# Sums of weight quarters for the feed-forwards' second matrices: from four VectorE additions to accumulating DMAs in DRAM, and three more tiles by seven products

## The chip, the core and the metric

The kernel runs on one core of a Trainium2 chip. Its time is device microseconds (us) from one launch; lower is better. Times below are either medians of several runs or come from one profiled execution, and it is said which.

## What is computed

A decoder layer for 512 tokens of width 1024, all in float32: a SwiGLU feed-forward (FFN1), a token mixer (HGRN2 and mLSTM heads), and a second feed-forward (FFN2), each between RMS norms and with a residual. Only the feed-forwards matter here:

```python
def swiglu_ffn(x, w_in, w_out):
    gate, up = jnp.split(x @ w_in, 2, axis=-1)
    return (jax.nn.silu(gate) * up) @ w_out        # (512, 2816) @ (2816, 1024)
...
    x = x + 0.5 * rms_norm(swiglu_ffn(rms_norm(x, norm_pre[l, 0]), ffn1_w_in[l], ffn1_w_out[l]), norm_post[l, 0])
    x = x + rms_norm(mixed, norm_post[l, 1])
    x = x + 0.5 * rms_norm(swiglu_ffn(rms_norm(x, norm_pre[l, 2]), ffn2_w_in[l], ffn2_w_out[l]), norm_post[l, 2])
```

## The kernel before

**Float32 by three matmuls.** Every float32 operand is split into a rounded high part and a low part (what is left). ScalarE (ACT) writes the high part with a copy, VectorE (DVE) the low part with a subtraction; `split` (L250, its instructions at L273 and L275) does this for each weight tile, `two_parts` (L812, L813) for each tile of activations. A product is then three matmuls: high by high, high by low, low by high.

**The second matrix (`ffn_out`, L858).** w_out has 2816 rows, taken in eleven pairs of 128 rows (k2 = 0 to 10), and 1024 columns, taken in two halves of 512. One tile is 256 rows by 512 columns, 512 KB. `OUT` gives the order of the pairs in each half; the last four (`LAST`) of the second half are done row chunk by row chunk, so that the norm after them can start early. A tile is done in one of two ways:

- *plain* (`plain`, L893): for each of four chunks of 128 tokens and each of two column quarters, two row halves by three matmuls of 128x256: 48 matmuls.
- *by quarters* (`product`, L901, called by `quartered`): the tile is taken as 2x2 quarters of 128 rows by 256 columns, and multiplied with seven products in place of eight (Strassen's scheme in Winograd's form), each of them two matmul columns by three matmuls: 42 matmuls. It needs four sums of the weight quarters and four sums of quarters of the activations. The activations' sums are DVE additions in `h_sums` (L844), split by `s_tile`; the plain quarters of the activations that it also needs are split by `h_quarters`. The weights' sums are four DVE additions of 128x256 in `sum_quarters` (L306), made in place in the loaded tile after its first split; then the tile is split a second time. So a quartered tile takes two entries of the list of weights, and its loaded buffer is held until the second one is split.

`QUARTERED` names the pairs done by quarters: six in the first half, four in the second. The products by quarters of one half go to four sums of their own (M), and `common` adds them to the results (C) once the last quartered tile of the half is done (L863); `post0` then takes the first half's results through square (ACT, L437), a small GpSimd (POOL) operation (L438) and a multiplication (DVE, L475).

**What sets the order.** All engines run their own queues in order. `weights` makes a due time for each load: a load can be issued when its ring buffer was read for the last time and not more than 8 entries ahead. Rings: `raw` with three buffers, `raw2` with five; all w_out tiles go through `raw2`. SyncE (SP) issues all loads in one queue (L236). `feed` keeps up to four split weight tiles (`WBUF`) ahead of TensorE (PE). Activations by quarters lie in the free buffers of the transposed input (`PLACES`), others in two of the three `raw` buffers. In `ffn_in` the first matrix goes through PE as products p1 to p7 of 24 matmuls each (L603); its weights are added up by DVE (L289) after their loads.

Of the kernel before, what the change touches and what calls it, by code (L numbers as in the profile page):

```python
# [8 lines left out]
F32 = mybir.dt.float32  # L9
F32R = mybir.dt.float32r  # L10
AF = mybir.ActivationFunctionType
ALU = mybir.AluOpType
PSUM = bass.MemoryType.PSUM

P = 128
T = 512
D = 1024
# [5 lines left out]
RAW, WBUF, PAD, LATE, NEXT, FRONT, STEP = 3, 4, 128, 112, 64, 96, 16  # L23
# [55 lines left out]

QUARTERED = [(2, 3, 4, 6, 7, 8), (2, 4, 6, 8)]
OUT = [list(range(PAIRS)), [9, 2, 4, 10, 6, 8, 0, 1, 3, 5, 7]]
LAST = 4
PLACES, LATER = {2: 1, 4: 2, 6: 0, 8: 3}, {0: (1, 0), 7: (2, 3)}

AGAIN, ROWS = (9, 10), (18, 19, 20, 21)

# [25 lines left out]
class Layer:  # L116
    def __init__(self, ctx, tc, aps):
        self.tc, self.nc = tc, tc.nc
        self.__dict__.update(aps)
        nc = self.nc  # L120
        pool = lambda name, **kw: ctx.enter_context(tc.tile_pool(name=name, bufs=1, **kw))
        self.cp, self.wp, self.sp, self.psp = pool("cp"), pool("wp"), pool("sp"), pool("psp", space=PSUM)
        self.uid, self.hold = 0, ()
        self.wt, self.free, self.slot = None, deque(), {}

        self.ident = self.cp.tile([P, P], F32, name="ident")
        make_identity(nc, self.ident)
        self.nhalf = self.cp.tile([P, 8], F32, name="nhalf")
        nc.gpsimd.memset(self.nhalf, -0.5)
        self.xs = self.cp.tile([P, NT, D], F32, name="xs")  # L130

        xq = {n: self.cp.tile([P, 2 * D + 2 * STEP * (n == 0)], F32R, name=f"xq{n}") for n in (1, 2, 3, 0)}
        self.xt = [xq[n] for n in range(4)]
        self.xq = [t[:, : 2 * D].rearrange("p (b k t) -> p b k t", b=2, k=KH) for t in self.xt]

        x0 = self.xt[0].rearrange("p (b x) -> p b x", b=2)[:, :, :D].rearrange("p b (k t) -> p b k t", k=KH)
        self.xh = [x0, *self.xq[1:]]
        self.prm = self.cp.tile([P, 36], F32, name="prm")

    def nm(self, s):  # L140
        self.uid += 1
# [108 lines left out]
    def split(self):  # L250

        nc = self.nc
        it = self.items.popleft()
        raw = self.raw[it.key]
        _, a, b = raw.shape
        if it.dst:
            w = it.dst()
        else:
            if self.wt is None:
                self.wt = self.wp.tile([P, 2 * D * WBUF + FRONT + PAD], F32R, name="w")  # L260
            if not self.slot and it.key[0] != "mix":
                self.free = deque(FREE2 if it.key[0] == "f2" else FREE)
            n, o = self.lie("out" if it.key[1] == "out" else "mix" if it.key[0] == "mix" and b == 512 else "any")
            self.free.remove(n)
            w = self.wt[:, o : o + 2 * D].rearrange("p (b k t) -> p b k t", b=2, k=a)
            self.slot[id(w)] = n, o, w
        hi, lo = self.both(w)
        if it.sums:
            raw, hi, lo = (self.flat(v)[:, QUARTER:] for v in (raw, hi, lo))
        self.ready.append((w, it.dst is not None))  # L270
        rows = it.rows
        if rows is None:
            nc.scalar.copy(hi, raw)  # L273
            yield
            self.low = nc.vector.tensor_tensor(lo, raw, hi.bitcast(F32), op=ALU.subtract)  # L275
        else:
            for j in range(a):
                nc.scalar.activation(hi[:, j], raw[:, j], AF.Copy, scale=rows[:, j : j + 1])
            yield
            for j in range(a):  # L280
                nc.vector.scalar_tensor_tensor(  # L281
                    lo[:, j], raw[:, j], rows[:, j : j + 1], hi[:, j].bitcast(F32), op0=ALU.mult, op1=ALU.subtract
                )
        with self.behind(*self.hold):
            for out, other in it.adds:
                o, c = self.raw[out], self.raw[other]

                late = out[1] >= (HEAD if out[0] == "f1" else 1)
                (nc.vector if late else nc.gpsimd).tensor_tensor(o, o, c, op=ALU.add)  # L289
        if it.sums:  # L290
            self.sum_quarters(self.quarters(self.raw[it.key]))
        self.load_due(self.done)
        self.done += 1
        yield
# [4 lines left out]
    def quarters(self, v):  # L299
        v = self.flat(v)  # L300
        return [v[:, QUARTER * j : QUARTER * (j + 1)] for j in range(4)]

    def sum_quarters(self, b):

        for out, a, c in ((1, 1, 0), (0, 0, 2), (2, 1, 2), (3, 2, 3)):
            self.nc.vector.tensor_tensor(b[out], b[a], b[c], op=ALU.add)  # L306

    def both(self, w):

# [472 lines left out]

    def ffn_in(self):

        for p, t in ORDER2[len(HEADS2) :] if self.second else ORDER[len(HEADS) :]:
            with self.behind(*(self.c22 if p == "p3" and self.second else ())):
                self.feed()
            self.c22 = []
            self.lag()
            self.prod(p, t)  # L790
            self.after(p, t)
            if t == PAIRS - 1 and p in ("p3", "p7"):
                self.hs.append(self.h_tile(len(self.hs)))
        self.feed()
        self.lag()
# [26 lines left out]
    def h_quarters(self, k2, n=None):  # L822

        src = self.by_chunk(k2)
        parts = self.x_place(n) if n is not None else [
            self.wp.tile([P, D], F32R, tag="raw", bufs=RAW, name=self.nm("once"))[:, P - 2 * STEP :] for _ in range(2)
        ]
        parts = [v[:, : 3 * QUARTER].rearrange("p (k c t) -> p k c t", c=2, t=P) for v in parts]
        self.two_parts(*(v[:, 0] for v in parts), src[:, 0, 1])
        self.two_parts(*(v[:, 1:] for v in parts), src[:, 1])  # L830
        return [[None] + [v[:, j] for j in range(3)] for v in parts]
# [5 lines left out]
    def h_sums(self, k2, stay):  # L837

        a = self.by_chunk(k2)
        f = self.hf[:, 2 * k2 : 2 * k2 + 2, :]  # L840
        if not stay:
            f = self.sp.tile([P, 2, T], F32, tag="xn", bufs=1, name=self.nm("hsum"))
        v = f.rearrange("p k (c u t) -> p k u c t", u=2, t=P)
        tt = lambda out, x, y, op: self.nc.vector.tensor_tensor(out, x, y, op=op)  # L844
        tt(v[:, 0, 0], a[:, 0, 1], a[:, 0, 0], ALU.subtract)
        tt(v[:, 1, 0], v[:, 0, 0], a[:, 1, 0], ALU.add)
        for k in range(2):
            tt(v[:, k, 1], a[:, k, 1], v[:, 1, 0], ALU.subtract)
        return f

    def s_tile(self, f):

        parts = self.s_place()
        self.two_parts(*parts, f)
        parts = [t.rearrange("p k (c u t) -> p k u c t", u=2, t=P) for t in parts]
        return [[t[:, j // 2, j % 2] for j in range(4)] for t in parts]

    def ffn_out(self, gpost_row, scale, after, trans, head):  # L858

# [46 lines left out]
        def quartered(C, M, a, s, begin):  # L906

            quarter = lambda t, j: [self.quarters(t[:, b])[j] for b in range(2)]
            A, S = (lambda j: [a[0][j], a[1][j]]), (lambda j: [s[0][j], s[1][j]])
            w = self.pull()  # L910
            product(M["p1"], A(1), quarter(w, 1), begin)
            product(C[1][1], A(3), quarter(w, 3), False)
            product(C[1][0], S(3), quarter(w, 2), False)
            self.drop(w)
            v = self.pull()
            product(M["p7"], S(0), quarter(v, 0), begin)
            product(M["p5"], S(1), quarter(v, 1), begin)
            product(M["p6"], S(2), quarter(v, 2), begin)
            product(C[0][1], A(2), quarter(v, 3), False)
            self.drop(v)  # L920

        def common(M, t):
# [21 lines left out]
        for half in range(2):  # L944
            C = [[self.ps() for _ in range(2)] for _ in range(2)]
            M, T, left = None, None, len(QUARTERED[half])
            for m, k2 in enumerate(OUT[half][: PAIRS - LAST * half]):
# [10 lines left out]
                else:  # L958
# [6 lines left out]
                            add(C, T, i % 2)  # L965
                    self.drop(w)
                n += 1
                if n == 1:
                    self.prod("p4", PAIRS - 1)
                    self.after("p4", PAIRS - 1)  # L970
# [104 lines left out]
    def ffn_items(self, name, w_in, w_out):  # L1075
# [47 lines left out]
        for h in range(2):  # L1123
            for k2 in OUT[h]:
                src = w_out[k2 * 2 * P : (k2 + 1) * 2 * P, h * 512 : (h + 1) * 512].rearrange("(k p) d -> p k d", p=P)
                key = (name, "out", h, k2)
                made.append(Item(key, [Load(key, src, 2, 512, "raw2", 5, 8)], sums=k2 in QUARTERED[h]))
                if k2 in QUARTERED[h]:
                    made.append(Item(key, ()))
                if h == k2 == 0:  # L1130
                    made.append(Item((name, PAIRS - 1, "a"), ()))
        return made
# [696 lines left out]
```

## Time and profile before

| | us |
|---|---|
| median of three runs (936.38, 938.04, 938.09) | 938.04 |
| the profiled execution's own time | 936.35 |
| its span, first to last instruction | 934.6 |

The prediction quotes the profile's lines. Line numbers are those of the kernel before. "PE ps L603 x24" is a group of 24 matmuls of line 603 that write a PSUM tile; "out<-in" are the program's names of the buffers. An idle time in brackets stands with what ended it. A matmul's own duration includes its way through the array, so that two in a row overlap; the rate is read from the start of one group to the start of the next.

### The profile page before, as it was taken

Reading aid. Unit: us, or ns where it says so; the run is one execution under the profiler, and the core shown is the slowest. Engines: PE = TensorE matmul, PEld = TensorE weight load, DVE = VectorE, ACT = ScalarE, POOL = GpSimd, SP = SyncE. Lnnn points to the kernel's source line nnn. Section 1 sums busy time; section 2 is a strip of 40 time slices with the busy share of each in tenths; the row PEclk is TensorE's granted clock in tenths of the full one; section 3 lists DMA queues with packets and bytes.
Section 4 is the critical chain, followed back from the end, with each engine's and each line's share of the span. In section 5 each row is a group of like instructions: output and inputs, shape, how many; then the busy total and the mean of one; then the engine's idle time right before and its main releaser. Section 6 shows DMA issues by size and latency. Waiting matters only on the chain.

```text
span 934.6 us, 18052 instructions
## 1 busy us (share of the span) xinstructions
PE 926.2 (99%) x7471; PEld 891.8 (95%) x7471; DVE 772.1 (83%) x1044; ACT 511.4 (55%) x735; POOL 106.5 (11%) x172
## 2 busy tenths in 40 slices
PE   9999999999999999999999999999999999999997
PEld 7999999999999999998887887899999999999997
DVE  6899988889988877698766565799899889998884
ACT  7645454557456466956533445595454545655541
POOL 3530000000001045200010310313000000000101
PEclk9999999999999999999999999999999999999999
DMA  9253343332352025421212124352354435334212
GB/s 313 94 157 91 119 132 113 93 112 71 114 177 91 24 72 134 114 70 54 81 46 69 46 91 150 98 181 70 112 158 136 136 116 159 111 91 126 79 46 91
DMA packets 86956, 101.35 MB, mean 108 GB/s; under 512 B 4277, under 2 KB 66777, under 8 KB 86874
## 3 DMA queue, kind: packets, MB, share of 16 engines
q1 hardware_dynamic: 86586, 99.68, 34.9%
q8 instruction: 58, 0.95, 0.4%
q10 hardware_dynamic: 288, 0.52, 0.2%
q14 instruction: 24, 0.20, 0.1%
HBM read 98.10 MB, written 2.10 MB: 107 GB/s over the span
## 4 chain that ended last, share of the span: by engine, by line
PE 62%; ACT 1%; issue 0%; DVE 0%; POOL 0%; DVEq 0%; POOLq 0%; ACTq 0%
PE ps L603 22%; PE ps L893 7%; PE ps L533 6%; PE ps L901 5%; PE ps L179 5%; PE ps L181 5%; PE ps L180 5%; PE ps L1307 2%; PE ps L348 1%; PE ps L543 1%; PE ps L1488 0%; PE ps L1399 0%; PE ps L1600 0%; PE ps L1573 0%; PE ps L1353 0%; PE ps L1597 0%
## 5 line engine op out<-in xcount | busy, mean ns | idle before, releaser
L273 ACT CAST w<-raw 128x1024 fp32r<-128x1024 f32 (+1 forms) x238 | 244.4, 1035 | 231.7 <-PE ps L603 92.8
L275 DVE TENSOR_TENSOR w<-raw,w 128x1024 fp32r<-128x1024 f32 (+1 forms) x238 | 290.9, 1229 | 38.0 <-ACT w L273 37.5
L603 PE MATMUL ps<-xq,w 128*128 128x256 f32 x2016 | 237.1, 277 | 0.0
L603 PEld LDWEIGHTS ps<-xq,w 128*128 128x128 f32 x2016 | 232.9, 188 | 0.0
L603 PE MATMUL ps<-sq,w 128*128 128x256 f32 x1512 | 178.0, 276 | 0.3
L603 PEld LDWEIGHTS ps<-sq,w 128*128 128x128 f32 x1512 | 174.3, 188 | 1.1 <-ACT ps L654 0.9
L893 PE MATMUL ps<-w,hs 128*128 128x256 f32 x960 | 113.0, 276 | 0.0
L893 PEld LDWEIGHTS ps<-w,hs 128*128 128x128 f32 x960 | 110.7, 188 | 0.0
L289 DVE TENSOR_TENSOR raw<-raw,raw 128x1024 f32<-128x1024 f32 x72 | 89.8, 1251 | 8.3 <-DMA raw<-in_ffn_w_in_dram 6.7
L179 PE MATMUL ps<-w,xq 128*128 128x512 f32 x192 | 78.0, 407 | 0.1
L180 PE MATMUL ps<-w,xq 128*128 128x512 f32 x192 | 74.9, 391 | 0.0
L181 PE MATMUL ps<-w,xq 128*128 128x512 f32 x192 | 74.9, 392 | 0.0
L438 POOL TENSOR_SCALAR col<-col 128x1 f32<-128x1 f32 x24 | 8.3, 347 | 513.4 <-ACT junk L437 513.3
L901 PE MATMUL ps<-w,hs 128*128 128x256 f32 x480 | 57.7, 276 | 0.0
L901 PEld LDWEIGHTS ps<-w,hs 128*128 128x128 f32 x480 | 55.9, 188 | 0.0
L533 PE MATMUL ps<-xq,w 128*128 128x256 f32 x480 | 55.7, 278 | 0.0
L533 PEld LDWEIGHTS ps<-xq,w 128*128 128x128 f32 x480 | 54.9, 188 | 0.5 <-issue 0.5
L179 PEld LDWEIGHTS ps<-w,xq 128*128 128x128 f32 x192 | 36.1, 188 | 8.5 <-issue 0.9
L181 PEld LDWEIGHTS ps<-w,xq 128*128 128x128 f32 x192 | 36.0, 188 | 8.0 <-DVE xq L355 0.3
L812 ACT CAST hs<-hf 128x1024 fp32r<-128x1024 f32 x32 | 33.7, 1052 | 17.5 <-PE ps L901 10.8
L180 PEld LDWEIGHTS ps<-w,xq 128*128 128x128 f32 x192 | 36.1, 188 | 7.3 <-DVE w L281 0.3
L813 DVE TENSOR_TENSOR hs<-hf,hs 128x1024 fp32r<-128x1024 f32 x32 | 39.0, 1217 | 1.3 <-ACT hs L812 1.2
(259 smaller groups left out, 1136.8 us busy)
## 6 DMA issues: line engine op xcount, KB each, us to landing
raw<-in_ffn_w_in_dram SPq DMA_DIRECT2D x98, 512.0 KB, 3.7
raw<-in_ffn_w_out_dram SPq DMA_DIRECT2D x44, 512.0 KB, 4.3
raw<-in_w_mix_in_dram SPq DMA_DIRECT2D x28, 512.0 KB, 3.7
raw<-in_w_mix_out_dram SPq DMA_DIRECT2D x8, 512.0 KB, 3.9
out_dram<-xs SPq DMA_DIRECT2D x8, 256.0 KB, 2.0
xs<-in_x_dram SPq DMA_DIRECT2D x6, 256.0 KB, 4.5
gpost<-in_norm_post_dram SPq DMA_DIRECT2D x3, 512.0 KB, 3.6
gpre<-in_norm_pre_dram SPq DMA_DIRECT2D x2, 512.0 KB, 4.8
```

What stands on the lines that cost most here:

```text
L179: mm(ps, sh, mh, start=start, stop=False, **kw)
L180: mm(ps, sh, ml, start=False, stop=False, **kw)
L181: mm(ps, sl, mh, start=False, stop=stop, **kw)
L273: nc.scalar.copy(hi, raw)
L275: self.low = nc.vector.tensor_tensor(lo, raw, hi.bitcast(F32), op=ALU.subtract)
L289: (nc.vector if late else nc.gpsimd).tensor_tensor(o, o, c, op=ALU.add)
L533: mm(ps[:, u0:u1], w[:, a, k, :], self.xop(k, b, u0, u1), start=k + n + m == 0, stop=k == ND - 1 and n == 2, skip_group_check=True,)
L603: self.nc.tensor.matmul(ps[:, c], wb[b][:, k, v], left[d][:, k, :], start=first and a + n + k == 0, stop=n == 2 and k == KH - 1, skip_grou ...
L812: self.nc.scalar.copy(hi, src)
L813: self.nc.vector.tensor_tensor(lo, src, hi.bitcast(F32), op=ALU.subtract)
L893: mm(out, a[kk][:, i * P : (i + 1) * P], w[:, b, kk, QUARTER * v : QUARTER * (v + 1)], start=begin and c == kk == n == 0, stop=kk == 1 and ...
L901: mm(ps[:, QUARTER * c : QUARTER * (c + 1)], A[a][:, c], B[b], start=begin and c == n == 0, stop=n == 2, skip_group_check=True,)
```

## The change

The four sums of weight quarters are no longer made by DVE. For each quartered tile a buffer in DRAM of 128 x 4 x 256 (512 KB) is added. `sums_ahead` fills it: three copies from DRAM to DRAM on SP's queue (quarter 1, quarter 2, quarters 2 and 3), queued behind the last load, and then three DMAs from GpSimd's queue that add while they write: quarter 0 onto the first two parts, the first part onto the third, the third onto the fourth. Each of the three waits for the one before it. `make_sums` starts one tile and takes the tiles in work one step on; it is called at every fifth product of `ffn_in` from the sixteenth on and after every other tile of the first half of `ffn_out`. The second entry of a quartered tile then has a load of its own, of the sums, through the same ring of five.

With this, eight tiles of the first half are done by quarters and five of the second. The lists of places, of tiles whose split activations are used again (`AGAIN`: now pair 10 alone) and the order of the second half change with it. Of the three pairs that are quartered in the first half alone (`APART`: 5, 7, 9) the low part of the quarters lies in the buffer of the norm's gains (`gpre`), so that their high part needs one `raw` buffer; pair 3 holds two `raw` buffers until its tile in the second half is done, and the next norm's gains are loaded after pair 9. The last two of the four additions in `h_sums` become one of twice the size.

```diff
-QUARTERED = [(2, 3, 4, 6, 7, 8), (2, 4, 6, 8)]
-OUT = [list(range(PAIRS)), [9, 2, 4, 10, 6, 8, 0, 1, 3, 5, 7]]
-LAST = 4
-PLACES, LATER = {2: 1, 4: 2, 6: 0, 8: 3}, {0: (1, 0), 7: (2, 3)}
-AGAIN, ROWS = (9, 10), (18, 19, 20, 21)
+QUARTERED = [(2, 3, 4, 5, 6, 7, 8, 9), (2, 3, 4, 6, 8)]
+OUT = [list(range(PAIRS)), [10, 2, 4, 3, 6, 8, 9, 0, 1, 7, 5]]
+LAST, APART = 4, (5, 7, 9)
+PLACES, LATER = {2: 1, 4: 2, 6: 0, 8: 3}, {7: (2, 3)}
+AGAIN, ROWS = (10,), (18, 19, 20, 21)
+EVERY = 5
...
-        if it.sums:
-            self.sum_quarters(self.quarters(self.raw[it.key]))
...
-    def sum_quarters(self, b):
-        for out, a, c in ((1, 1, 0), (0, 0, 2), (2, 1, 2), (3, 2, 3)):
-            self.nc.vector.tensor_tensor(b[out], b[a], b[c], op=ALU.add)
...
+        for n, (p, t) in enumerate(ORDER2[len(HEADS2) :] if self.second else ORDER[len(HEADS) :]):
+            if n > 14 and n % EVERY == 0:
+                self.make_sums()
...
-        parts = self.x_place(n) if n is not None else [
-            self.wp.tile([P, D], F32R, tag="raw", bufs=RAW, name=self.nm("once"))[:, P - 2 * STEP :] for _ in range(2)
-        ]
+            places = [(self.wp, "raw", RAW, P - 2 * STEP), (self.cp, "gpre", 1, STEP // 2)]
+            parts = [once(*places[k2 in APART and m]) for m in range(2)]
...
-        for k in range(2):
-            tt(v[:, k, 1], a[:, k, 1], v[:, 1, 0], ALU.subtract)
+        tt(v[:, :, 1], a[:, :, 1], v[:, 1:2, 0].broadcast_to([P, 2, 2, P]), ALU.subtract)
...
+    def sums_ahead(self, f, h, k2):
+        nc, to = self.nc, self.sums_of[f, h, k2]
+        w = (self.ffn1_w_out, self.ffn2_w_out)[f == "f2"][0]
+        q = w[k2 * 2 * P : (k2 + 1) * 2 * P, h * 512 : (h + 1) * 512].rearrange("(k p) (c f) -> p k c f", p=P, f=QUARTER)
+        with self.behind(self.loaded):
+            nc.sync.dma_start(to[:, 0], q[:, 0, 1])
+            nc.sync.dma_start(to[:, 1], q[:, 1, 0])
+            nc.sync.dma_start(to[:, 2:], q[:, 1])
+        yield
+        for a, b, v in ((0, 2, q[:, 0, :1].broadcast_to([P, 2, QUARTER])), (2, 3, to[:, :1]), (3, 4, to[:, 2:3])):
+            nc.gpsimd.dma_start(to[:, a:b], v, accum_op=ALU.add)
+            yield
+    def make_sums(self):
+        if self.ahead:
+            self.making.append(self.sums_ahead(*self.ahead.popleft()))
+        self.making = [g for g in self.making if next(g, self) is not self]
...
+                if half == 0 and n % 2:
+                    self.make_sums()
...
-                made.append(Item(key, [Load(key, src, 2, 512, "raw2", 5, 8)], sums=k2 in QUARTERED[h]))
-                if k2 in QUARTERED[h]:
-                    made.append(Item(key, ()))
+                four = k2 in QUARTERED[h]
+                made.append(Item(key, [Load(key, src, 2, 512, "raw2", 5, 8)], sums=four))
+                if four:
+                    key, src = (*key, "sums"), self.sums_of[name, h, k2].rearrange("p (a j) f -> p a (j f)", a=2)
+                    made.append(Item(key, [Load(key, src, 2, 512, "raw2", 5, 8)]))
```

More of the change, by code (lines that the diff above doesn't have):

```diff
@@ L138, in __init__ @@
         self.prm = self.cp.tile([P, 36], F32, name="prm")
+        dram = ctx.enter_context(tc.tile_pool(name="sums", bufs=1, space=bass.MemoryType.DRAM))
+        self.sums_of = {
+            (f, h, k2): dram.tile([P, 4, QUARTER], F32, name=f"{f}sums{h}_{k2}")
+            for f in ("f1", "f2") for h in range(2) for k2 in OUT[h] if k2 in QUARTERED[h]
+        }
     def nm(self, s):
@@ L783, in ffn_in @@
     def ffn_in(self):
-        for p, t in ORDER2[len(HEADS2) :] if self.second else ORDER[len(HEADS) :]:
+        self.ahead = deque(fhk for fhk in self.sums_of if fhk[0] == ("f2" if self.second else "f1"))
+        self.making = []
+        for n, (p, t) in enumerate(ORDER2[len(HEADS2) :] if self.second else ORDER[len(HEADS) :]):
+            if n > 14 and n % EVERY == 0:
+                self.make_sums()
             with self.behind(*(self.c22 if p == "p3" and self.second else ())):
@@ L824, in h_quarters @@
         src = self.by_chunk(k2)
-        parts = self.x_place(n) if n is not None else [
-            self.wp.tile([P, D], F32R, tag="raw", bufs=RAW, name=self.nm("once"))[:, P - 2 * STEP :] for _ in range(2)
-        ]
+        once = lambda pool, tag, bufs, o: pool.tile([P, D], F32R, tag=tag, bufs=bufs, name=self.nm("once"))[:, o:]
+        if n is not None:
+            parts = self.x_place(n)
+        else:
+            places = [(self.wp, "raw", RAW, P - 2 * STEP), (self.cp, "gpre", 1, STEP // 2)]
+            parts = [once(*places[k2 in APART and m]) for m in range(2)]
         parts = [v[:, : 3 * QUARTER].rearrange("p (k c t) -> p k c t", c=2, t=P) for v in parts]
@@ L914, in quartered @@
             self.drop(w)
[L915 to L919, printed above, removed]
+            v, at = self.pull(), (1, 0, 2, 3)
+            product(M["p7"], S(0), quarter(v, at[0]), begin)
+            product(M["p5"], S(1), quarter(v, at[1]), begin)
+            product(M["p6"], S(2), quarter(v, at[2]), begin)
+            product(C[0][1], A(2), quarter(v, at[3]), False)
             self.drop(v)
```

## The prediction

> **What bounds the kernel now.** I read the page's head and its chain first, then the stages by windows, then single groups in order of time.
>
> ```profile
> span 934.6 us, 18052 instructions
> PE 926.2 (99%) x7471; PEld 891.8 (95%) x7471; DVE 772.1 (83%) x1044; ACT 511.4 (55%) x735; POOL 106.5 (11%) x172
> PEclk9999999999999999999999999999999999999999
> q1 hardware_dynamic: 86586, 99.68, 34.9%
> PE 62%; ACT 1%; issue 0%; DVE 0%; POOL 0%; DVEq 0%; POOLq 0%; ACTq 0%
> ```
>
> PE is busy for 99% of the span at full clock, and the chain that ended last is PE wherever it names an engine at length. So a matmul removed is time removed, as long as the others keep up. Whether they do is seen in the stages of the feed-forwards (columns: time busy and number of instructions of PE, weight load, DVE, ACT, POOL; clock; DMA share; GB/s):
>
> ```profile
> 60.00:224.00 164.00, 164.00 (x1446) 164.00 (x1445) 149.03 (x162) 88.96 (x112) 0.00 (x0) 1.00 0.38 117
> 224.00:288.00 64.00, 64.00 (x567) 64.00 (x567) 58.56 (x94) 33.27 (x50) 2.44 (x8) 1.00 0.41 124
> 620.00:800.00 180.00, 179.67 (x1574) 178.91 (x1573) 166.85 (x175) 94.25 (x119) 11.42 (x4) 1.00 0.42 128
> 800.00:900.00 100.00, 100.00 (x885) 100.00 (x884) 90.89 (x136) 60.26 (x83) 2.44 (x8) 1.00 0.32 101
> ```
>
> PE has no gap there, but DVE is at 91 to 93%, POOL is nearly idle, and the DMA engines are 32 to 42% busy. DVE is the engine that could become the bound; the DMA engines have room.
>
> **The change part by part.**
>
> *Matmuls.* The price of a tile is read from the starts of the groups in FFN1's first half:
>
> ```profile
> 237.64 1.52 PE L901 MATMUL ps<-w,xq 128*128 128x256 f32 x12
> 239.00 2.88 PE L901 MATMUL ps<-w,hs 128*128 128x256 f32 x24
> 241.72 0.84 PE L901 MATMUL ps<-w,xq 128*128 128x256 f32 x6
> 242.40 1.52 PE L901 MATMUL ps<-w,once 128*128 128x256 f32 x12
> 251.92 5.60 PE L893 MATMUL ps<-w,hs 128*128 128x256 f32 x48
> 257.36 1.52 PE L901 MATMUL ps<-w,xq 128*128 128x256 f32 x12
> ```
>
> A quartered tile takes 242.40 - 237.64 = 4.76 us for 42 matmuls, a plain one 257.36 - 251.92 = 5.44 us for 48: 0.1133 us each, 0.68 us less per tile. In the built order the plain matmuls go from 1152 to 864 and those of quartered tiles from 840 to 1092: 36 fewer, six tiles, three in each feed-forward. That is 6 x 0.68 = **4.08 us** off the path. It certainly happens; all that follows is what may take it back.
>
> *DVE and ACT.* The durations, from the second matrix of FFN1:
>
> ```profile
> L306 DVE TENSOR_TENSOR raw<-raw 128x256 f32<-128x256 f32 x40 | 16.9, 422 | 0.8
> L813 DVE TENSOR_TENSOR hs<-hf,hs 128x1024 fp32r<-128x1024 f32 x16 | 19.5, 1218 | 0.6 <-ACT hs L812 0.6
> L275 DVE TENSOR_TENSOR w<-raw,w 128x768 fp32r<-128x768 f32 x10 | 9.5, 950 | 0.0
> L844 DVE TENSOR_TENSOR hf<-hf 128x256 f32<-128x256 f32 x13 | 5.4, 418 | 0.2
> L813 DVE TENSOR_TENSOR once<-hf,once 128x512 fp32r<-128x512 f32 x2 | 1.4, 682 | 0.0
> ```
>
> Per feed-forward DVE loses the 40 sums, 16.9 us. It gains three more splits of 0.95, one split of activations of 1.22, two more `h_quarters` of 0.42 + 0.68, and in `h_sums` 8 x (2 x 0.42 + 0.68) in place of 6 x 4 x 0.42, 2.1 more: 8.4 us. Net -8.5 us, of which about -4 in the first half, where DVE is fullest. ACT gains about 5.5 us per feed-forward and is at 52 to 60%. Neither changes the time by itself, since PE did not wait for them; it pays for delays elsewhere.
>
> *The loads.* Each quartered tile now takes two buffers of the ring of five, one after the other, in place of one held long. In a run of quartered tiles the buffer of entry k is refilled for entry k+5, five entries or 5 x 2.38 = 12 us later; the load needs about 4.3 us (row below). Cover remains about 6 us.
>
> *The making of the sums.* Per feed-forward 39 copies on SP and 39 adding DMAs on POOL. On SP the copies stand behind a load that is already issued and wait for no engine, but the next loads in the same queue run behind their bytes. On POOL nothing else stands in the queue until the squares of the first half are taken, so an adding DMA goes out as soon as the one before it has landed. No row shows an adding DMA, so I bound a step from rows:
>
> ```profile
> raw<-in_ffn_w_out_dram SPq DMA_DIRECT2D x44, 512.0 KB, 4.3
> out_dram<-xs SPq DMA_DIRECT2D x8, 256.0 KB, 2.0
> graw<-in_w_mix_in_dram SPq DMA_DIRECT2D x1, 32.0 KB, 6.7
> ```
>
> From below 2.0 us (256 KB written to DRAM); from above 6.7 us (a small transfer in short runs). A step adds 128 or 256 KB and has to read both sides, so the 512 KB load is nearest: I take 4.3 us, 13 us a tile. The tightest place is the end of FFN2's first half. The last four tiles' sums (pairs 4, 3, 6, 8 of the second half) are 12 steps in POOL's queue, and behind them stand the L438 operations; ACT's squares need their column buffers back, and behind the squares on ACT stand the next weights' splits.
>
> ```profile
> 209.33 0.37 SPq L236 DMA_DIRECT2D raw<-in_ffn_w_out_dram  x1
> 224.04 5.60 PE L893 MATMUL ps<-w,hs 128*128 128x256 f32 x48
> 806.47 0.37 SPq L236 DMA_DIRECT2D raw<-in_ffn_w_out_dram  x1
> 812.99 5.44 PE ps L893 x48
> 282.06 0.19 POOL L438 TENSOR_SCALAR col<-col 128x1 f32<-128x1 f32 x1 [224.75 <-ACT junk L437]
> 285.09 2.38 DVE L475 TENSOR_TENSOR y<-ps,gpost 128x256 f32<-128x256 f32 x6
> 287.96 1.52 PE L901 MATMUL ps<-w,xq 128*128 128x256 f32 x12
> ```
>
> The first of the four copies stands behind the load issued at 806.5, so it lands at about 811. The first half runs from 813.0 for 8 x 4.76 + 3 x 5.44 + 2.72 (p4, 24 matmuls) = 57 us to 870, and then PE has four split weight tiles: a plain pair, a quartered one and 18 matmuls of a third, 12 us. 12 x 4.3 = 52 us ends at 863: in time, at no cost.
>
> *The turn between the halves.* Before, two plain tiles (10.9 us) lay between the last quartered tile and the second half, now one (5.44 us). In it ACT copies one sum and DVE does four operations of `common`, some 3.5 us with the split beside them; then `post0` as before. Before, DVE's last y ended at 287.5 and PE took the banks at 287.96 without a gap: half a us of cover. I take 0.3 us lost per feed-forward, **+0.6 us**; bounds 0 and 2 x 1.5 us (the whole of what moved beyond its cover).
>
> *Gains' buffer, `raw` buffers, reuse lists.* The activations of pair 7 wait for pair 5, of 9 for 7, both a tile (4.76 us) before they are needed, for 0.42 + 0.68 us on DVE after at most two splits of 1.2: about 1.5 us spare, no cost; if it went, the same 1.5 us would be late. The gains' load moves from the start to after pair 9, still a whole half ahead of its use.
>
> *The sum* against the profiled execution: 936.35 - 4.08 + 0.6 = **932.9 us**. The median shown, 938.04, is 1.7 us above that execution, and the lowest run equals it; so the median after should lie between 932.9 and 934.6, and I give **933.5 us**.
>
> *A rule weighed.* GpSimd and DVE can exclude each other:
>
> ```profile
> 51.48 5.82 POOL L289 TENSOR_TENSOR raw<-raw,raw 128x1024 f32<-128x1024 f32 x2 [1.16 <-DVE col L1149]
> 52.59 2.36 DVE L1150 TENSOR_TENSOR col<-prm,col 128x4 f32<-128x4 f32 x1
> 54.87 0.15 DVE L1151 TENSOR_TENSOR col<-prm,col 128x4 f32<-128x4 f32 x1
> ```
>
> A DVE addition of 128x4 took 2.36 us beside a POOL addition, and its like 0.15. If POOL's issue of an adding DMA did this too, it would be the third rival below. The Trainium skill, "SBUF — State Buffer", section "Who interferes with whom", says that a DVE instruction with two SBUF inputs contends with a GpSimd instruction that reads SBUF and not with one that only writes it. By that rule an issue, which only writes descriptors, would cost DVE nothing and the sum would stay; the trace agrees with the exclusion but has no such issue to show. The Trainium skill, "DMA: Bandwidth & Descriptors", section "Anatomy of one DMA — SWDGE (gpsimd) path", gives 2.0 us plus bytes at 436 GB/s, which as an estimate is 2.3 to 2.6 us a step and would end the twelve steps at about 840.
>
> **The rivals.**
>
> *Late loads in FFN2 (no change).* In FFN1 past its start the view of waits names no load; in FFN2 it does:
>
> ```profile
> 750.14 0.37 SPq L236 DMA_DIRECT2D raw<-in_ffn_w_in_dram  x1
> 753.14 0.37 SPq L236 DMA_DIRECT2D raw<-in_ffn_w_in_dram  x1
> 754.27 0.94 SPq L236 DMA_DIRECT2D raw<-in_ffn_w_in_dram  x1
> 759.65 1.23 DVE L289 TENSOR_TENSOR raw<-raw,raw 128x1024 f32<-128x1024 f32 x1 [2.54 <-DMA raw<-in_ffn_w_in_dram]
> 764.99 2.00 ACT L273 CAST w<-raw 128x1024 fp32r<-128x1024 f32 x2 [1.93 <-DVE raw L289]
> ```
>
> DVE already waited 2.54 us for the load of 754.27, and the copies of pair 7 now go out between the loads of 750.14 and 753.14. At the rate of q1 (99.68 MB in 34.9% of 934.6 us, 306 GB/s) a copy of 512 KB takes 1.7 us and the adding about twice that. Two to three us more of waiting are within the three products (8 us) by which splits run ahead of PE, and DVE catches up; but at 93% it does so slowly. Eight sets of copies fall there; if they cost PE 3 us in all, the time is 932.9 + 3 = 936, which with the shift of the median is no change.
>
> *The adding chain is late (slower).* The 12 steps have from 811 until PE runs out of split weights at 882: 5.9 us a step in FFN2, and 6.6 in FFN1, where the first of the copies stands behind the load of 209.33, 14.7 us ahead of its half (224.04), and not 6.5. From there each us more costs 12 us in each. At 7 us, the upper row, that is 13 + 5 us: 932.9 + 18 = 951 us. For it: the 6.7 us row, and that a step reads what it writes. Against it: 4.3 us for a load of four times a 128 KB step.
>
> *POOL's issue holds DVE (slower).* In the 57 us of the first half DVE's idle (5.4 of 64 us) and the 4 us it is spared make about 9 us for some 15 steps: from 0.6 us a step DVE is the bound. At half a POOL addition (1.2 us) it is 15 x 0.6 = 9 us in each feed-forward: 932.9 + 18 = 951 us.
>
> That the change does not do what it says can be left out: the 36 matmuls are gone from the built order.
>
> **How the numbers follow.** About 0.2% is what a measurement can tell from no change: 1.9 us. Forecast 0.60; late loads 0.16; late chain 0.15; held DVE 0.06; anything else slower 0.03. The forecast is faster; of late loads nearly all is within 0.2%; the rest is slower. So faster 0.60, same 0.17, slower 0.23. The range begins at 931.0: all of the 4.08 us from the lowest run, 932.3, less 1.3, as three runs of one kernel differ by 1.7 us. It ends at 944, inside the slower rivals, since their losses begin at nothing and grow; some 0.2 is left out.
>
> **What would show it.** Right: 36 fewer matmuls, L306 gone, PE's rows at 4.76 us without gaps, DVE below 90% in the first half, adding DMAs landing within 5 us, and the L438 operations right behind ACT's squares. Wrong: ACT or SP waiting for POOL or for an adding DMA, a DVE wait for a load in FFN2 well above 2.5 us with PE idle behind it, or DVE operations above 1.25 us for 128x1024 beside POOL.

## The result: slower by 0.6%, and the profile after

The changed kernel took 943.49 us (median of six runs, 942.49 to 944.06), the kernel before 937.6 us in the same comparison: a ratio of 1.0062, 95% interval 1.0049 to 1.0075. The forecast was faster, 933.5 us. The time lies in the range given; the direction was wrong.

The profiled execution has a span of 941.3 us, 6.7 us more than before. First where they lie. These are starts of groups of matmuls in the timeline of PE, before:

```profile
602.17 2.99 PE L603 MATMUL ps<-xq,sq 128*128 128x256 f32 x24
812.82 5.60 PE L893 MATMUL ps<-w,hs 128*128 128x256 f32 x48
927.74 0.84 PE L893 MATMUL ps<-w,xq 128*128 128x256 f32 x6
```

and after (line 602 is a product of the first matrix, 918 a plain tile of the second):

```profile
225.25 5.60 PE L918 MATMUL ps<-w,hs 128*128 128x256 f32 x48
601.40 2.98 PE L602 MATMUL ps<-xq,sq 128*128 128x256 f32 x24
820.18 5.60 PE L918 MATMUL ps<-w,hs 128*128 128x256 f32 x48
933.06 0.84 PE L918 MATMUL ps<-w,hs 128*128 128x256 f32 x6
```

| stretch | before | after | difference |
|---|---|---|---|
| to the start of FFN1's second matrix | 224.04 | 225.25 | +1.21 |
| from there to the start of FFN2 | 378.13 | 376.15 | -1.98 |
| FFN2's input product | 210.65 | 218.78 | **+8.13** |
| FFN2's second matrix, to its last group | 114.92 | 112.88 | -2.04 |
| from there to the end of the span | 6.86 | 8.24 | +1.38 |

The removed matmuls brought in each feed-forward what was forecast. FFN2's input product took back twice that, the end of the span 1.4 us, and the start 1.2 us (the last of these is within what a second run of the kernel before moves by itself, see below).

The page's lines that answer to those of before:

```profile
span 941.3 us, 18295 instructions
PE 925.5 (98%) x7435; PEld 890.5 (95%) x7435; DVE 758.8 (81%) x980; ACT 521.6 (55%) x751; POOL 182.2 (19%) x250
q1 hardware_dynamic: 101562, 126.95, 43.6%
q0 software_dynamic: 14560, 13.64, 11.2%
PE 50%; DVE 7%; issue 3%; DMA 2%; POOL 1%; ACT 1%; DVEq 0%; POOLq 0%; ACTq 0%
raw<-in_ffn_w_in_dram SPq DMA_DIRECT2D x98, 512.0 KB, 6.4
```

DVE is less busy (758.8 in place of 772.1 us) and yet stands in the chain with 7%, and DMA with 2%; before, the chain was PE's with 62%, and no other engine had more than 1%. q0 is new: it is the adding DMAs. They moved 13.64 MB in 11.2% of the span, q1 moved 126.95 MB in 43.6%: 0.82% per MB against 0.34%, so here a byte that is added kept the DMA engines 2.4 times as long. The median landing of the first matrix's loads went from 3.7 us to 6.4.

The view of waits of PE, and of DVE for a load (total, times, longest):

```profile
PE ps L602 <- DVE ps L621: 6.1, 3, 2.6
```

```profile
DVE raw L295 <- DMA raw<-in_ffn_w_in_dram: 15.7, 6, 4.1
```

Before, the same row of DVE was:

```profile
DVE raw L289 <- DMA raw<-in_ffn_w_in_dram: 6.7, 4, 2.5
```

PE names no split weights (line 281) here but L621, an addition of DVE into a PSUM bank. The timeline of DVE shows how a late load gets there:

```profile
747.32 1.22 DVE L295 TENSOR_TENSOR raw<-raw,raw 128x1024 f32<-128x1024 f32 x1
752.68 1.23 DVE L295 TENSOR_TENSOR raw<-raw,raw 128x1024 f32<-128x1024 f32 x1 [4.15 <-DMA raw<-in_ffn_w_in_dram]
753.83 1.22 DVE L281 TENSOR_TENSOR w<-raw,w 128x1024 fp32r<-128x1024 f32 x1
...
758.56 1.22 DVE L281 TENSOR_TENSOR w<-raw,w 128x1024 fp32r<-128x1024 f32 x1
759.74 1.22 DVE L295 TENSOR_TENSOR raw<-raw,raw 128x1024 f32<-128x1024 f32 x1
760.89 0.69 DVE L621 TENSOR_TENSOR ps<-ps,hf 128x512 f32<-128x512 f32 x1
```

and that of PE:

```profile
761.73 2.48 PE L602 MATMUL ps<-sq,w 128*128 128x256 f32 x19 [2.56 <-DVE ps L621]
```

An addition of two loaded weight tiles (L295) waits 4.15 us for its load. DVE's queue is in order, so all that follows waits too, and from 752.68 on DVE works without a gap and does not catch up before PE needs the bank at 759. The product accumulates on what L621 writes, so PE stands 2.56 us.

The three stops, read from the starts of the groups, come to 6.6 us of the 8.13. The other 1.5 us are in the matmuls behind them, as after the first stop:

```profile
709.12 3.06 PE L602 MATMUL ps<-sq,w 128*128 128x256 f32 x24 [1.20 <-DVE ps L621]
712.02 2.99 PE L602 MATMUL ps<-xq,w 128*128 128x256 f32 x24
```

This group of 24 took 2.90 us from start to start; before, at the same place, it took 2.72. The granted clock reads 1.00 in this stretch, so the cause of the slower groups is not shown. In other runs the clock itself fell at a stop (below), and four of the six timed runs of the change list a mean granted clock of 0.994 or 0.995, where the profiled one has 0.998.

### The profile page after: what moved, and what is told of

It is laid out like the page before. It is cut to its first block, busy times and chain, and to the rows that moved or that the text cites. A ratio compares the mean times of both kernels' runs of the same rounds, so it can differ in the third digit from the quotient of the medians.

```text
span 941.3 us, 18295 instructions
## 1 busy us (share of the span) xinstructions
PE 925.5 (98%) x7435; PEld 890.5 (95%) x7435; DVE 758.8 (81%) x980; ACT 521.6 (55%) x751; POOL 182.2 (19%) x250
## 3 DMA queue, kind: packets, MB, share of 16 engines
q1 hardware_dynamic: 101562, 126.95, 43.6%
q0 software_dynamic: 14560, 13.64, 11.2%
## 4 chain that ended last, share of the span: by engine, by line
PE 50%; DVE 7%; issue 3%; DMA 2%; POOL 1%; ACT 1%; DVEq 0%; POOLq 0%; ACTq 0%
PE ps L602 11%; PE ps L926 7%; PE ps L532 6%; PE ps L918 5%; PE ps L185 5%; PE ps L187 5%; PE ps L186 5%; DVE w L281 4%; DMA raw<-in_ffn_w_in_dram 2%; PE ps L1336 2%; DVE raw L295 1%; PE ps L347 1%; POOL raw L295 1%; PE ps L542 1%; DVE ps L621 1%
## 5 line engine op out<-in xcount | busy, mean ns | idle before, releaser
L279 ACT CAST w<-raw 128x1024 fp32r<-128x1024 f32 x244 | 249.7, 1030 | 197.3 <-PE ps L602 93.8
L281 DVE TENSOR_TENSOR w<-raw,w 128x1024 fp32r<-128x1024 f32 x244 | 297.2, 1222 | 31.9 <-ACT w L279 30.7
L295 DVE TENSOR_TENSOR raw<-raw,raw 128x1024 f32<-128x1024 f32 x72 | 89.9, 1252 | 17.2 <-DMA raw<-in_ffn_w_in_dram 15.7
L918 PE MATMUL ps<-w,hs 128*128 128x256 f32 x768 | 91.2, 276 | 0.0
L918 PEld LDWEIGHTS ps<-w,hs 128*128 128x128 f32 x768 | 88.9, 188 | 0.0
L926 PE MATMUL ps<-w,hs 128*128 128x256 f32 x624 | 74.9, 276 | 0.0
L926 PEld LDWEIGHTS ps<-w,hs 128*128 128x128 f32 x624 | 72.7, 188 | 0.0
L815 ACT CAST hs<-hf 128x1024 fp32r<-128x1024 f32 x34 | 35.8, 1054 | 31.5 <-PE ps L926 19.7
L816 DVE TENSOR_TENSOR hs<-hf,hs 128x1024 fp32r<-128x1024 f32 x34 | 41.5, 1222 | 10.1 <-ACT hs L815 9.8
L874 POOL DMA_DIRECT2D f2sums<-f2sums x26 | 21.6, 832 | 132.1 <-DMA f2sums<-in_ffn_w_out_dram 83.4
L185 PEld LDWEIGHTS ps<-w,xq 128*128 128x128 f32 x192 | 36.1, 188 | 8.4 <-issue 0.9
L187 PEld LDWEIGHTS ps<-w,xq 128*128 128x128 f32 x192 | 36.0, 188 | 8.1 <-DVE xq L354 0.3
L874 POOL DMA_DIRECT2D f1sums<-f1sums x26 | 21.8, 840 | 112.7 <-DMA f1sums<-in_ffn_w_out_dram 54.9
```

Of the source, the lines that this page charges most:

```text
L185: mm(ps, sh, mh, start=start, stop=False, **kw)
L187: mm(ps, sl, mh, start=False, stop=stop, **kw)
L816: self.nc.vector.tensor_tensor(lo, src, hi.bitcast(F32), op=ALU.subtract)
L874: nc.gpsimd.dma_start(to[:, a:b], v, accum_op=ALU.add)
L918: mm(out, a[kk][:, i * P : (i + 1) * P], w[:, b, kk, QUARTER * v : QUARTER * (v + 1)], start=begin and c == kk == n == 0, stop=kk == 1 and ...
L926: mm(ps[:, QUARTER * c : QUARTER * (c + 1)], A[a][:, c], B[b], start=begin and c == n == 0, stop=n == 2, skip_group_check=True,)
```

## The experiments

**Theory L:** the adding DMAs of FFN2's sums, made during its input product, keep the DMA engines from the loads of the first matrix; DVE waits for these, and PE for DVE. **Rivals:** the copies do it, by their bytes or by the time SP takes to issue them; POOL's issues hold DVE up; what is late is the second loads of the quartered tiles or the new order, whatever makes the sums.

### Without FFN2's making

```diff
-        self.ahead = deque(fhk for fhk in self.sums_of if fhk[0] == ("f2" if self.second else "f1"))
+        self.ahead = deque(fhk for fhk in self.sums_of if fhk[0] == "f1" and not self.second)
...
-                    key, src = (*key, "sums"), self.sums_of[name, h, k2].rearrange("p (a j) f -> p a (j f)", a=2)
+                    key = (*key, "sums")
+                    if not second:
+                        src = self.sums_of[name, h, k2].rearrange("p (a j) f -> p a (j f)", a=2)
```

> FFN2's copies and adding DMAs are left out, and its second loads read the plain quarters, so the output is not the layer's; FFN1 and every matmul, split and load of FFN2 stay. Theory L (late loads): in FFN2's input product the making takes the DMA engines from loads that are used 3.5 to 8 us after their issue, and PE stood 6.6 us there (1.36 + 2.72 + 2.50). Then these gaps go and the time falls from 943.5 to 937 us. Rival S (the seven and eight more matmul groups, or the second loads themselves, are what is late): the gaps stay, 943 us. End of the span: before, POOL answered SP's last drain after 0.04 us, after the change 1.32 us. If any adding DMA in the program does that, 1.3 us stay (FFN1 still has 39); if the last one has to lie near the end, they go too, 935.7 us.

Measured: 934.69 us, ratio to the kernel before 0.9972 (0.9963 to 0.9982). PE's waits in FFN2's input product went from 6.1 us to

```profile
PE ps L602 <- DVE ps L621: 0.4, 1, 0.4
```

So the making costs it, and not the second loads, whose number is unchanged here, nor the order. The time is 1.2 us above the 933.5 us of the forecast. The end of the span shrank too; it is taken up below.

### Without FFN2's adding DMAs, and with tiny copies

```diff
         yield
+        if f == "f2":
+            return
...
             nc.gpsimd.dma_start(to[:, a:b], v, accum_op=ALU.add)
```

> FFN2's 39 adding DMAs on POOL are left out, its 39 copies on SP stay (the output is not the layer's). If the adding DMAs' load on the DMA engines makes the loads late: under 2 us of the 6.6 us of gaps in FFN2's input product stay, 937 to 939 us. If the copies do it, by their bytes ahead of the loads in SP's queue or by the 1.7 us that SP takes to issue three of them: 4 us or more of the gaps stay, 941 to 943.5 us.

Measured: 935.22 us, ratio 0.9986 (0.9977 to 0.9994). The other way round, first in a form that went wrong:

```diff
+        if f == "f2":
+            to = self.sums_of["f1", h, k2]
-        with self.behind(self.loaded):
+        with self.behind(*[self.loaded] * (f == "f1")):
+          if f == "f1":
             nc.sync.dma_start(to[:, 0], q[:, 0, 1])
...
```

> FFN2's 39 copies on SP are left out, its 39 adding DMAs on POOL stay and write onto the buffers of FFN1 (the output is not the layer's). The mirror of the run without adding DMAs: if the adding DMAs make the loads late, 4 us or more of the 6.6 us stay, 941 to 943.5 us; if the copies do, under 2 us stay, 937 to 939 us. If each takes part and only the two together use up the slack of the loads, both runs are at 937 to 939 us.

Measured: 993.61 us, ratio 1.0603 (1.0590 to 1.0617), outside both expectations. Without copies nothing held FFN2's adding DMAs back, and they were queued on POOL in FFN1, ahead of the small operations of its norm. The run does not answer its question, but it prices the rival of the late adding chain: 

```profile
PE ps L929 <- DVE y L474: 54.3, 2, 53.2
```

```profile
ACT junk L436 <- POOL col L437: 59.7, 2, 57.4
```

ACT's squares waited for column buffers behind the adding DMAs, DVE's y for the squares, and PE for the banks: the path that the prediction named, at 53 us. The question was put again with copies in their places but with few bytes:

```diff
+            n = QUARTER if f == "f1" else 16
-            nc.sync.dma_start(to[:, 0], q[:, 0, 1])
+            nc.sync.dma_start(to[:, 0, :n], q[:, 0, 1, :n])
-            nc.sync.dma_start(to[:, 1], q[:, 1, 0])
+            nc.sync.dma_start(to[:, 1, :n], q[:, 1, 0, :n])
-            nc.sync.dma_start(to[:, 2:], q[:, 1])
+            nc.sync.dma_start(to[:, 2:, :n], q[:, 1, :, :n])
```

> The change as it is, but FFN2's copies take 16 of each 256 columns, a sixteenth of the bytes, at the same places in SP's queue, and FFN2's adding DMAs stay whole (the output is not the layer's). If the adding DMAs alone make the loads late, most of the 6.6 us of PE's gaps stays: 940 to 943 us. If it takes both, copies and adding, to use up the slack, the gaps fall under 2 us: 936 to 938 us.

Measured: 944.14 us, ratio 1.0072 (1.0054 to 1.0090), as the change itself. The three side by side, in the view of the loads' line (L242 or its like) from 690 to 800 us. The change, then without adding DMAs, then with tiny copies:

```profile
DMA to landing us min/median/max: 4.8/6.3/8.6
```

```profile
DMA to landing us min/median/max: 3.6/4.5/5.7
```

```profile
DMA to landing us min/median/max: 3.6/5.8/8.4
```

and before (there line 236):

```profile
DMA to landing us min/median/max: 3.5/3.7/5.0
```

PE's waits for L621 were 0.4 us without adding DMAs, and with tiny copies

```profile
PE ps L602 <- DVE ps L621: 6.3, 3, 2.8
```

The copies alone make a load 0.8 us later in the median, with 0.4 us of waiting on PE; the adding DMAs, with next to no copied bytes, do what the whole change does. SP's issuing and the copies' bytes fall out as causes. The DMA share from 690 to 800 us was 0.43 before, 0.55 with copies alone, 0.69 with adding DMAs and tiny copies, and 0.79 with both. No run tells whether the loads wait in the DMA engines or at the DRAM behind them.

### FFN2's sums in the mixer

In the mixer, from 380 to 480 us, POOL works for 2.6 us and the DMA share is 0.26 in the change. `plan_sums("f2")` is called in the mixer ahead of the loops over HGRN2's levels, and `fill`, which deals out PE's other work there, makes the sums on; the calls in FFN2 are gone.

```diff
+    def plan_sums(self, f):
+        self.ahead, self.making, self.fills = deque(fhk for fhk in self.sums_of if fhk[0] == f), [], 0
...
     def fill(self, n):
         for _ in range(n):
+            self.fills += 1
+            if self.fills % 5 == 0:
+                self.make_sums()
```

> All of the change stays, but FFN2's 39 copies and 39 adding DMAs are made during the mixer (span 380 to 480 us, DMA share 0.25, POOL idle) in place of FFN2's input product and first half. Theory L: PE's gaps in FFN2's input product go, as no work is missing: 943.5 - 6.6 = 937 us, or up to 3 us more if POOL's first own operation after the adding DMAs (the clearing of a buffer at 479 us) is held up and the mixer waits for it. Rival S: 943 us.

Measured: 943.51 us, ratio 1.0072 (1.0045 to 1.0099). This version counted in a variable that FFN1's input product also reads, so that FFN1's products were combined in another way (its output is not the layer's) and PE stood 3.2 us there, at 52 us, so that the time answers nothing. In FFN2's input product PE's waits for L621 were 0.8 us. Once more with a name of its own:

> As the run with FFN2's sums made in the mixer, but with FFN1 untouched (there a name in the code clashed and moved FFN1's additions too). All of the work is done. Theory L (FFN2's loads are late because of the adding DMAs): PE has no gap above 1 us in FFN2's input product and the time is that of the run without FFN2's making, 934.7, plus the longer end of the span (all 78 adding DMAs again: POOL's last drain 5.5 us, about 0.9 us more): 935.6 us, a little under the kernel before. Against L: a gap in FFN2's input product stays, or as much is lost in the mixer: 940 us or more.

Measured: 939.36 us, ratio 1.0021 (1.0003 to 1.0039), with single runs from 935.8 to 943.3 us. The profile is of one of the longer ones, 942.23 us. Of the 6.1 us of PE's waits in FFN2 0.5 were left; but in the mixer a new one came:

```profile
PE ps L1523 <- DVE pT L1525: 4.2, 1, 4.2
PE ps L602 <- DVE ps L621: 0.5, 1, 0.5
```

The timelines of POOL and of DVE tell why:

```profile
490.35 0.81 POOL L874 DMA_DIRECT2D f2sums<-f2sums  x1 [0.80 <-DMA f2sums<-in_ffn_w_out_dram]
493.99 1.65 POOL L874 DMA_DIRECT2D f2sums<-f2sums  x2 [2.83 <-DMA f2sums<-f2sums]
495.68 1.39 POOL L1548 MEMSET C<- 128x1548 f32 x1
497.03 1.24 POOL L1515 TENSOR_SCALAR_AFFINE_SELECT e<-e 128x512 f32<-128x512 f32 x2
497.71 0.69 DVE L1525 SCALAR_TENSOR_TENSOR pT<-ps,e 128x512 f32<-128x512 f32 x1 [9.46 <-POOL e L1515]
```

The clearing of C stood behind the last adding DMAs, each of which waits for the one before it, and behind it POOL's masking of e (L1515), for which DVE waited 9.46 us; in the change the clearing was at 479.55. PE's granted clock was 0.92 from 480 to 500 us and 0.91 from 500 to 520, so this stop cost more than its 4.2 us. Theory L holds in FFN2; the loss is the one in the mixer that the first of the two expectations named, and in this run larger than its 3 us. That the shorter runs, at 936 us, escaped it is likely, but none of them was profiled.

### In large pieces: in the mixer, and in place

FFN2's tiles are taken four at a time (pairs 2 to 5, 6 to 9, and 2, 4, 6, 8 of the second half), and pair 3 alone: 16 adding DMAs and 12 copies in place of 39 and 39.

```diff
+    def group_ahead(self, f, h, ks, to):
...
+            nc.sync.dma_start(to[:, :, 0], q[:, :, 0, 1])
...
+        for a, v in ((0, q[:, :, 0, 0]), (1, q[:, :, 0, 0]), (2, to[:, :, 0]), (3, to[:, :, 2])):
+            nc.gpsimd.dma_start(to[:, :, a], v, accum_op=ALU.add)
+            yield
```

> FFN2's sums in the mixer, made for four tiles (and once for one) at a time: 16 adding DMAs of 512 and 128 KB in place of 39, 12 copies in place of 39; the same sums and all of the layer. POOL's last drain took 0.66 us without any adding DMA, 3.87 us with 39, 5.50 us with 78: a straight line through the last two, 2.24 us and 0.042 us for each, gives 4.5 us with 55, so that it ends about where SP's last wait ends: 934.7 to 935.2 us, below the run with 78. If the drain does not go by the number of adding DMAs but by their bytes, 5.5 us and the same time as that run.

Measured: **934.72 us, ratio 0.9977 (0.9966 to 0.9988)**: it does all of the work and is faster than both kernels, than the one before by 0.23%, some 2 us. The last adding DMA was issued at 471.68, the clearing of C stands at

```profile
479.08 1.39 POOL L1570 MEMSET C<- 128x1548 f32 x1 [6.58 <-DVE sT L1369]
```

PE waited for no load any more; in the loads' line the landing is

```profile
DMA to landing us min/median/max: 3.4/3.4/4.1
```

The same pieces put back into FFN2's input product:

> FFN2's sums again in its own input product, but in the large pieces of the run that was fastest: 16 adding DMAs and 12 copies in place of 39 and 39, the same bytes. If the bytes that the adding DMAs put through the DMA engines make the loads late, PE's gaps in FFN2's input product stay at 4 us or more: 940 to 944 us. If the number of DMAs does it (their fixed cost on POOL and on the queues), the gaps fall under 2 us: 935 to 937 us.

Measured: 968.20 us, ratio 1.0331 (1.0309 to 1.0352), worse than either expectation:

```profile
PE ps L607 <- DVE ps L626: 29.0, 4, 15.5
```

```profile
DMA to landing us min/median/max: 3.9/16.0/17.8
```

The bytes are the same as in the change and the DMAs fewer; yet in the median a load from 690 to 800 us landed after 16 us. So neither the number nor the sum of the bytes sets the price. How long the transfers go on at a stretch beside a load that is due in 4 to 8 us fits all runs, but it is argued: the copies on SP's queue came in large pieces too (512 and 1024 KB), and no run separates them from the large adding DMAs. PE's waits for the same bytes went from nothing (mixer) through 6 us (spread, in place) to 29 us (in bursts, in place); the times are 934.72, 943.49 and 968.20 us.

The last step is 33.5 us from the mixer to bursts in place, more than the 29 us of waits, as PE also came back at a lower clock:

```profile
752.60 4.97 PE L607 MATMUL ps<-sq,w 128*128 128x256 f32 x24 [15.51 <-DVE ps L626]
757.41 2.94 PE L607 MATMUL ps<-xq,w 128*128 128x256 f32 x24
```

The first group after the stop took 4.81 us from start to start in place of 2.72, at a granted clock of 0.55 (view by windows, 752.6 to 757.4 us); behind it the clock was 1.00 again.

### The sums by DVE, the change again, the kernel before again

```diff
+        if it.sums:
+            self.sum_quarters(self.quarters(self.raw[it.key]))
-                    made.append(Item(key, [Load(key, src, 2, 512, "raw2", 5, 8)]))
+                    made.append(Item(key, ()))
```

> The change's order of tiles (eight and five by quarters, 36 matmuls fewer), but all sums made by DVE as before, no DMA adds or copies. In the first halves DVE was busy 55.4 of 64 us (FFN1) and 51.8 of 63 us (FFN2) with the sums in DRAM; 32 sums of 0.42 us are 13.5 us more, 68.9 and 65.3 us. If DVE then is the bound there, 2 to 5 us are lost in each feed-forward: 934 + 4 to 10 = 938 to 944 us. If the weights split ahead cover it: 934 us, and the sums need not have left DVE.

Measured: 944.71 us, ratio 1.0082 (1.0068 to 1.0096), with

```profile
PE ps L932 <- DVE w L281: 5.6, 8, 0.9
```

DVE was busy for 63.1 of the 64 us from 224 to 288 us, in FFN1's first half. So three more tiles by quarters do need the sums off DVE. What failed in the change is the place of the making, not the idea.

> The change once more, beside the others on one chip: 943 us, gaps of PE in FFN2's input product 6 to 7 us. Its first product started 12.63 us into the span, that of the kernel before 11.56 us; the runs without FFN2's making and without its adding had 12.70 and 11.89 us. If the change itself delays the start, 12.6 us again; if it is chance, anything from 11.6 to 12.7 us.

Measured: 943.87 us (939.2 to 945.9), ratio 1.0067 (1.0047 to 1.0088). Its profiled run was one of the shorter, with a span of 937.5 us and 3.5 us of PE's waits for L621: what the adding costs varies from run to run. That it hangs on which load meets which DMA is likely, but not shown.

> The kernel before, for a second profile. Its first product started at 11.56 us; the six profiles of kernels with the change's FFN1 had 11.91 to 12.70 us (one with another FFN1 11.67). If the start moves by chance from run to run, this one need not be at 11.56 us again; if it is, the change costs some 0.7 us at the start.

Measured: 938.96 us, one run, span 937.2 us, with its first product at 13.88 us. In the first profile it was at 11.56 us, in the change at 12.63. The start moves by chance by more than the 1.2 us of the table, so these can't be put down to the change.

## Why the prediction was wrong, point by point

- **Matmuls: right.** 4.08 us forecast; -1.98 and -2.04 us in the two stretches that hold the second matrices (the first of them holds the mixer too).
- **The turn between the halves: no cost.** 0.3 us per feed-forward was forecast; the 4.02 us leave 0.06 us for both. The buffers of `gpre` and `raw` and the reuse lists cost nothing either.
- **DVE: right in direction.** 13.3 us less in all, where 17 were forecast. That brought nothing by itself, as was said.
- **The step of an adding DMA: sized too low.** 4.3 us was taken. From the page's DMA rows, issue to landing:

```profile
f2sums<-in_ffn_w_out_dram POOLq DMA_DIRECT2D x13, 256.0 KB, 8.2
f2sums<-f2sums POOLq DMA_DIRECT2D x26, 128.0 KB, 4.7
```

  One of 8.2 and two of 4.7 are 5.9 us a step on average, just the 5.9 us that was given as the point from which the late chain decides. POOL issued twelve of them from 820.36 to 882.63 us, 5.7 us apart, where the sum had the last one done at 863. PE had no gap behind them, but ACT's squares did wait for POOL, which the prediction had named as a sign of this rival:

```profile
883.71 0.39 ACT L436 ACTIVATE junk<-ps 128x256 f32<-128x256 f32 x1 [3.29 <-POOL col L437]
```

  That this stayed without cost is partly luck: the chain used up the margin that the sum had seen, and PE itself came 7.2 us late to this half (820.18 in place of 812.99). In the second profile of the change, where PE came at 816.35, ACT waited 1.7 us and PE again not at all.

  The Trainium skill, "DMA: Bandwidth & Descriptors", section "Anatomy of one DMA — SWDGE (gpsimd) path", would have 2.3 and 2.6 us (an estimate by its 2.0 us plus bytes at 436 GB/s); the trace has about twice and three times that, and the measurement decides.
- **POOL's issue holding DVE: did not happen.** DVE's splits in the stretch from 690 to 760 us, before, and after with fifteen adding DMAs issued:

```profile
L275 DVE TENSOR_TENSOR w<-raw,w 128x1024 fp32r<-128x1024 f32 x25 | 30.4, 1216 | 0.6 <-ACT w L273 0.5
L281 DVE TENSOR_TENSOR w<-raw,w 128x1024 fp32r<-128x1024 f32 x24 | 29.2, 1219 | 0.2
```

  1219 ns beside 1216. The Trainium skill, "SBUF — State Buffer", section "Who interferes with whom", by which a GpSimd instruction that only writes SBUF leaves a two-input DVE instruction alone, agrees with these rows, if an issue only writes, as the prediction took it.
- **Late loads in FFN2: the step that failed.** The sum had this term at nothing. The mechanism stood among the rivals with a chance of 0.16 and a price of 3 us; it cost 8. The price rested on the sentence that "Two to three us more of waiting are within the three products (8 us) by which splits run ahead of PE". A single wait did grow by about that (the longest of DVE's for a load from 2.5 to 4.1 us; all of them from 6.7 us over four loads to 15.7 over six). But the split weights are not what PE reaches first. Behind the waiting addition in DVE's queue stands the operation that writes a PSUM bank on which one of PE's next products accumulates. Before, at the same place of the sequence:

```profile
754.16 1.22 DVE L289 TENSOR_TENSOR raw<-raw,raw 128x1024 f32<-128x1024 f32 x1
755.30 0.69 DVE L622 TENSOR_TENSOR ps<-ps,hf 128x512 f32<-128x512 f32 x1
```

```profile
757.30 2.88 PE L603 MATMUL ps<-sq,w 128*128 128x256 f32 x24
```

  L622 ended at 755.99 and PE began the product that accumulates on it at 757.30: 1.3 us of cover, not 8. These rows were there to be read. The loads' own cover was read at one place only (2.54 us of waiting already), and the DMA share of FFN2's input product, which went from 0.45 to 0.79 between 690 and 760 us, was not worked out at all:

```profile
690.00:760.00 70.00, 67.97 (x590) 67.60 (x588) 58.63 (x63) 34.19 (x41) 14.24 (x15) 1.00 0.79 193
```

- **The end of the span: not in the sum.** 1.38 us. POOL's last DRAIN, ahead of the barrier that ends the program, in the view of that line (ns, shortest, median and longest of three), after and before:

```profile
L1854 POOLq DRAIN  x3: 38/93/5502, 935.0 to 941.1; - x3
```

```profile
L1825 POOLq DRAIN  x3: 39/78/656, 929.7 to 934.4; - x3
```

  It begins behind POOL's last operation and took 5.5 us in place of 0.66; SP, which waits for the output to land, had its own done at 939.2, before the drain's end at 940.5.

FFN1 lost nothing, though its loads landed late too (3.6 to 9.9 us from 100 to 220 us, median 7.1): in that stretch the trace has 12 us or more from a load's issue to its use.

## What to carry to other kernels

A DMA that costs no time of a compute engine is still paid for where a load is due soon after its issue: before moving work to the DMA engines, set the slack from issue to use of the loads in that stretch beside the time of the new DMAs, and put these where slack is long. To price a late load, follow the waiting engine's own queue to the first instruction behind it that another engine needs; the cover is the slack of that one, not of the waiting instruction's own result. Where transfers could be made far ahead in an idle stretch, fewer and larger ones were better here, because the chain ended earlier; beside loads that were due, large ones were worst. And a stop of PE can cost more than its length: count the groups behind it too.

## What the runs showed of the hardware that was not expected

- Adding DMAs from DRAM to DRAM kept the DMA engines 2.4 times as long per byte as the transfers of SP's queue on average (0.82% and 0.34% of the span per MB, in the change's profile).
- A load of 512 KB that landed in 3.7 us (median) in the kernel before took up to 8.6 us beside adding DMAs of 128 and 256 KB and copies of the same sizes, and 16 us in the median, 17.8 at most, beside adding DMAs of 512 KB and copies of 512 and 1024 KB.
- After stops of PE the granted clock was lower for a while in some runs: 0.55 in the 4.8 us behind a stop of 15.5 us (bursts in place), 0.50 from 498.5 to 501.5 us behind one of 4.2 us (mixer, small pieces), and a mean of 0.97 from 690 to 800 us with stops of up to 2.8 us (tiny copies). In the change's own profile, with stops of up to 2.6 us, it stayed at 1.00.
- POOL's last drain is longer once POOL has issued DMAs, even hundreds of microseconds earlier: 0.66 us without any, 3.87 us with FFN1's 39, 5.50 us with 78 small ones. It does not go by their number or bytes: with 55, which moved the same bytes as the 78, it took 3.79 us, where the straight line of the expectation gave 4.5. What sets it stays open.
